# A decoder block whose output projection goes from seven products of halves to plain products by column tiles

## The chip, the cores and the metric

The kernel runs as one program on one core of a Trainium2 chip. The metric is the device time of one execution in microseconds (us). Engines are named as in the profile: PE (TensorE) multiplies, PEld is its loading of weights, DVE is VectorE, ACT is ScalarE, POOL is GpSimd, and SP issues the transfers (DMA).

## The reference

One decoder layer over 1024 tokens of width 1024. An input projection feeds three groups of token mixers (sparse attention with 8 heads of 64, a convolution of 256 channels, gated linear attention of 256 values). Their results, 1024 columns in all, go through ONE output projection and are added to the residual stream; then come a gated FFN of width 2816, a gated embedding and a last norm. The part that matters here:

```
x = x + concatenate([y_nsa, y_conv, y_gla]) @ w_out         # 1024 x 1024 @ 1024 x 1024
h = rms_norm(x, ffn_norm_g)                                 # x * rsqrt(mean(x*x) + eps) * g
x = x + (silu(h @ ffn_w_gate) * (h @ ffn_w_up)) @ ffn_w_down
```

## The kernel before

**Layout and precision.** The residual stream is held transposed: 8 tiles of 128 rows (columns of the model) by 1024 tokens. A float32 operand is split in a high part (a cast on ACT, L1043) and a low part (a subtraction, L271, on VectorE, or on POOL while the counter `pool_lo` is above 0), and every product of two operands is three matmuls: high x high (L1054), high x low (L1055), low x high (L1056). `split` (L1041) makes such a pair of parts from 128 x 512 values. A "product" of the text is one such 128 x 128 by 128 x 512 matmul.

**Seven products for eight.** The output projection works on pairs of column tiles, the two halves of the inner dimension (4 tiles of 128 each) and the two halves of the tokens, as 2 x 2 blocks, and forms seven block products in place of eight from sums and differences of blocks. `Right` (L1058) makes the seven operands on the token side ("11", "21", "22" and the sums "t1" to "t4", 4 splits each; t1, t2 and t4 are subtracted in place on VectorE, t3 on POOL). `Pair` (L1079) loads two tiles of weights, makes the weight sums on POOL (L1105 and L271) and the seven block products of 12 matmuls each, in four banks, with copies of intermediate results (L1095, L1116, L1126, L1135) and sums of them on POOL (L1136, L1137). `residual` (L1163) then adds the blocks to x, with 3 additions on VectorE and 4 on POOL for each pair (L1169), stores x, squares it on ACT (L1187) and adds the squares to sqs, one half on VectorE and one on POOL, and scales x by the norm's gain (L1190) to a "raw" tile, in place for the first three pairs. The FFN's gate and up projections use the same two classes, with the raws as the right side: `Right(raws[:4], raws[4:])` after the projection, then "11", the first product of two pairs, "t1", the fifth product, "21", and so on.

**Order.** The inner dimension is turned round so that the convolution and the linear attention come first (tiles 0 to 3, loaded from a buffer `ycg`) and the attention heads last (tiles 4 to 7). `out_steps` (L1146) is a generator that is advanced while the last units of attention drain: it makes "11", the first products of two pairs, "t1" and the fifth products, 48 matmuls that need only tiles 0 to 3. After attention come a third pair's first product, "21", the second products, and the rest. The instructions of every engine are put in order ahead of time by a scheduler, which may take a later instruction first when it is ready, so that operands of the FFN are begun while the projection still runs. The order of each engine is then fixed. Tiles live in a set of 46 slots of 4 KB for each partition (and four smaller ones), assigned by a dry run of the program; eight banks of PSUM are used in turn.

Of the kernel before, what the change touches and what calls it, by code (L numbers as in the profile page):

```python
# [12 lines left out]
AF = mybir.ActivationFunctionType  # L13
ALU = mybir.AluOpType
# [6 lines left out]
P = 128  # L21
NT = S // P
KT = D // P
# [59 lines left out]
RINGS = ((0, 3), (3, 7), (7, 8))  # L83
LOOK = 3
EARLY = 2
SQE = "vp"
RES = "pppp"
DPL = 7
D3 = True
RAWIN = 3  # L90
FIFTH = 2
DEPTH = 3
LATE = (2, 1, 1)
# [129 lines left out]
def tile_block(ctx: ExitStack, tc: tile.TileContext, a: dict, out: bass.AP, plan: Plan):  # L223
    nc = tc.nc
    mm = nc.tensor.matmul
# [17 lines left out]
    def B(name, dt=F32, shape=(P, 1024)):  # L243
        return place(name, shape, dt)
# [4 lines left out]
    def M(n, shape, dt=F32):  # L249
        return place(f"m{n}", shape, dt)  # L250
# [42 lines left out]
    pv = {n: par[:, s:e] for n, (s, e) in PAR.items()}  # L293
# [127 lines left out]
    ycg = dram.tile([4, P, S], F32, name="ycg")  # L421
# [120 lines left out]
    ps = mtile(4)  # L542
# [122 lines left out]
    for i in range(2):  # L665
        ps = mtile(5 + i)
# [54 lines left out]
    for t in range(NT):  # L721
        ps = row_tile(wV, 280, t)
        if t % 2 == 0:
            V.append(B("V", F32R, (P, 2, 4, P)))
        v = V[-1][:, t % 2]
# [141 lines left out]
    for br in range(2):  # L867
        ps = B("kv")
# [172 lines left out]
    def split(src):  # L1041
        o = B("op", F32R, (P, 2, 512))
        nc.scalar.copy(o[:, 0, :], src)  # L1043
        sub(nc.gpsimd if pool_lo[0] > 0 else nc.vector, o[:, 1, :], src, f(o[:, 0, :]))
        pool_lo[0] -= 1
        return o

    def half(x, n):
        return x[:, n * 512:(n + 1) * 512]
# [8 lines left out]
    class Right:  # L1058
# [5 lines left out]

        def make(self, *names):
            for k, (l, u) in enumerate(zip(self.lower, self.upper)):
                b11, b12, b21, b22 = half(l, 0), half(l, 1), half(u, 0), half(u, 1)
                for n in names:
                    if n == "t1":
                        sub(nc.vector, b11, b12, b11)  # L1070
                    if n == "t2":
                        sub(nc.vector, b11, b22, b11)
                    if n == "t3":
                        sub(nc.gpsimd, b12, b22, b12)
                    if n == "t4":
                        sub(nc.vector, b11, b21, b11)
                    self.x[n][k] = split({"21": b21, "22": b22, "t3": b12}.get(n, b11))
# [63 lines left out]

    x1d = dram.tile([KT, P, S], F32, name="x1d")
    actd = dram.tile([MF, P, S], F32, name="actd")
    outs = []

    def out_steps():  # L1146
        for kt in range(4, 8):
            nats[kt] = B("nat")
            nc.sync.dma_start(out=nats[kt], in_=ycg[kt - 4])
        r = Right([nats[4 + k] for k in range(4)], [nats[k] for k in range(4)])  # L1150
        outs.append(r)
        pool_lo[0] = DPL
        r.make("11")
        for c in range(2):
            outs.append(Pair(a["w_out"], 2 * c, r))
            outs[-1].first(False)
            yield
        r.make("t1")
        for p in outs[1:3]:
            p.fifth()  # L1160
            yield

    def residual(p, c):  # L1163

        for u in range(2):
            m = 2 * c + u
            x = B("x1")
            nc.sync.dma_start(out=x, in_=a["xT"][m])
            add = lambda eng, o, i: eng.tensor_tensor(out=o, in0=i, in1=o, op=ALU.add)  # L1169
            x0, x1_ = half(x, 0), half(x, 1)  # L1170
            if u == 0:
                add(nc.vector, x0, p.a)
                add(nc.vector, p.p6, p.c)
                add(by[RES[0]], x1_, p.p6)
            else:
                add(nc.vector, p.p1, p.b)
                add(by[RES[1]], x0, p.p1)
                add(by[RES[2]], p.p5, p.p67)
                add(by[RES[3]], x1_, p.p5)
            nc.sync.dma_start(out=x1d[m], in_=x)  # L1180
            if m == 0:
                sqs.append(B("sqs"))
                nc.scalar.activation(sqs[0], x, AF.Square)
            else:
                for k in range(2):
                    sq = M(2, (P, 512))
                    nc.scalar.activation(sq, half(x, k), AF.Square)  # L1187
                    add(by[SQE[k]], half(sqs[0], k), sq)
            raws.append(x if c < RAWIN else B("raw"))
            nc.scalar.activation(raws[m], x, AF.Copy, scale=pv["ffng"][:, m:m + 1])  # L1190

    raws, sqs = [], []
    by = {"v": nc.vector, "p": nc.gpsimd}

    nxt = iter(())
    pend = []
# [26 lines left out]
        products(*fifo.pop(0))  # L1223
    pump(og)
    pool_lo[0] = 0
    r = outs.pop(0)
    if D3:
        outs.append(Pair(a["w_out"], 4, r))
        outs[-1].first(False)
    r.make("21")  # L1230
    for p in outs:
        p.second()
    r.make("t2")
    outs[0].sixth()
    r.make("t3", "22", "t4")
    for c in range(KT // 2):
        if c >= len(outs):
            outs.append(Pair(a["w_out"], 2 * c, r))
            outs[c].first()
        outs[c].rest()  # L1240
        residual(outs[c], c)


    r = Right(raws[:4], raws[4:])
    r.make("11")
    pairs = {}
    for q in range(EARLY):
        pairs[q // 2, q % 2] = Pair(a["w_u" if q % 2 else "w_g"], q // 2 * 2, r)
        pairs[q // 2, q % 2].first(False)
    r.make("t1")  # L1250
    for q in range(FIFTH):
        pairs[q // 2, q % 2].fifth()
    r.make("21")
# [65 lines left out]
    def add(o, i0, eng=nc.vector):  # L1319
        eng.tensor_tensor(out=o, in0=i0, in1=o, op=ALU.add)  # L1320
# [244 lines left out]
```

## Time and profile before

| | |
|---|---|
| median of 3 runs | 1473.82 us (1468.57 to 1473.93) |
| profiled execution, its time | 1475.02 us |
| profiled execution, its span | 1473.2 us |
| mean granted TensorE clock | 0.975 |
| busy share PE / PEld / DVE / ACT / POOL | 95 / 79 / 73 / 47 / 58% |
| bytes moved | 118.37 MB, 80 GB/s |

The span runs from the first to the last instruction; the execution's own time is 1.8 us longer. A busy share is an average over all stages. A matmul's own time (about 0.4 us) is longer than the distance to the next one, as matmuls are pipelined; the distance is what counts. The granted clock is a share of 2.4 GHz.

### The profile page before, as it was taken

Reading aid. Unit: us, or ns where it says so; the run is one execution under the profiler, and the core shown is the slowest. Engines: PE = TensorE matmul, PEld = TensorE weight load, DVE = VectorE, ACT = ScalarE, POOL = GpSimd, SP = SyncE. Lnnn points to the kernel's source line nnn. Section 1 sums busy time; section 2 is a strip of 40 time slices with the busy share of each in tenths; the row PEclk is TensorE's granted clock in tenths of the full one; section 3 lists DMA queues with packets and bytes.
Section 4 is the critical chain, followed back from the end, with each engine's and each line's share of the span. In section 5 each row is a group of like instructions: output and inputs, shape, how many; then the busy total and the mean of one; then the engine's idle time right before and its main releaser. Section 6 shows DMA issues by size and latency. Waiting matters only on the chain.

```text
span 1473.2 us, 19463 instructions
## 1 busy us (share of the span) xinstructions
PE 1393.6 (95%) x7032; PEld 1166.6 (79%) x7032; DVE 1072.9 (73%) x1767; ACT 687.5 (47%) x1337; POOL 849.6 (58%) x778
## 2 busy tenths in 40 slices
PE   8999999999999989878899999999996999999998
PEld 6898777889998977756688888888874877876886
DVE  3896548468998978698766666566659999988533
ACT  7322522448887876554433333333334343544532
POOL 3850533548887785986565556665678659423111
PEclk9999999999999999987999999999999999999999
DMA  9101022400000031421222221222263522221211
GB/s 359 56 15 48 26 67 69 148 0 9 5 5 8 2 119 43 172 100 43 72 86 86 86 73 70 73 87 86 86 236 115 182 94 78 105 93 46 69 54 43
DMA packets 40783, 118.37 MB, mean 80 GB/s; under 512 B 4532, under 2 KB 9326, under 8 KB 40686
## 3 DMA queue, kind: packets, MB, share of 16 engines
q1 hardware_dynamic: 40542, 117.11, 22.9%
q8 instruction: 55, 0.90, 0.3%
q14 instruction: 42, 0.34, 0.1%
q10 hardware_dynamic: 144, 0.01, 0.0%
HBM read 94.03 MB, written 23.08 MB: 79 GB/s over the span
## 4 chain that ended last, share of the span: by engine, by line
PE 61%; DVE 17%; POOL 10%; ACT 4%; issue 4%; DMA 3%; SPq 0%; POOLq 0%; DVEq 0%; ACTq 0%
DVE op L271 10%; PE banks L1054 6%; PE banks L1056 6%; PE banks L1055 6%; PE banks L970 3%; PE banks L375 3%; PE banks L376 3%; PE banks L372 3%; POOL st L271 3%; ACT op L1043 3%; PE banks L1014 2%; PE banks L1015 2%; PE banks L910 2%; PE banks L1462 2%; PE banks L1460 2%
## 5 line engine op out<-in xcount | busy, mean ns | idle before, releaser
L1054 PE MATMUL banks<-op 128*128 128x512 f32 x728 | 285.5, 399 | 20.4 <-ACT op L1043 10.4
L1055 PE MATMUL banks<-op 128*128 128x512 f32 x728 | 288.8, 397 | 5.4 <-DVE op L271 5.4
L1056 PE MATMUL banks<-op 128*128 128x512 f32 x728 | 284.8, 397 | 3.1 <-DVE op L271 3.0
L1410 PE MATMUL banks<-op 128*128 128x512 f32 x924 | 220.4, 398 | 23.2 <-DVE x L1320 10.2
L1410 PEld LDWEIGHTS banks<-op 128*128 128x128 f32 x924 | 175.8, 192 | 67.3 <-DVE op L271 10.5
L271 DVE TENSOR_TENSOR op<-nat,op 128x512 fp32r<-128x512 f32 x179 | 176.1, 1001 | 46.1 <-ACT op L1043 44.0
L1043 ACT CAST op<-nat 128x512 fp32r<-128x512 f32 x186 | 111.7, 620 | 178.7 <-DVE op L271 82.8
L1054 PEld LDWEIGHTS banks<-op 128*128 128x128 f32 x728 | 139.4, 192 | 55.0 <-ACT op L1043 13.4
L1056 PEld LDWEIGHTS banks<-op 128*128 128x128 f32 x728 | 139.5, 192 | 35.4 <-DVE op L271 6.2
L1055 PEld LDWEIGHTS banks<-op 128*128 128x128 f32 x728 | 139.8, 192 | 34.8 <-DVE op L271 5.9
L271 DVE TENSOR_TENSOR op<-ws,op 128x512 fp32r<-128x512 f32 x104 | 109.4, 1057 | 78.4 <-ACT op L1043 76.1
L925 POOL TENSOR_SCALAR p<-p,sums,gates 128x640 f32<-128x640 f32 (+7 forms) x128 | 99.9, 791 | 38.6 <-DVE sums L921 29.0
L1043 ACT CAST op<-ws 128x512 fp32r<-128x512 f32 x104 | 63.8, 620 | 108.5 <-POOL ws L271 74.7
L916 ACT ACTIVATE p<-p,mn 128x640 f32<-128x640 f32 (+7 forms) x128 | 94.7, 742 | 11.8 <-DVE mn L913 11.7
L372 PE MATMUL banks<-hT,whi 128*128 128x512 f32 x208 | 84.7, 408 | 6.9 <-ACT hT L328 6.4
L375 PE MATMUL banks<-hT,whi 128*128 128x512 f32 x208 | 84.4, 406 | 0.5 <-DVE hT L329 0.5
L376 PE MATMUL banks<-hT,wlo 128*128 128x512 f32 x208 | 83.0, 401 | 0.0
L970 PE MATMUL banks<-cst,p 128*128 128x128 f32 x448 | 72.1, 279 | 6.8 <-DVE pt L271 4.5
L271 DVE TENSOR_TENSOR op<-st,op 128x512 fp32r<-128x512 f32 x66 | 70.4, 1080 | 9.4 <-ACT op L1043 8.5
L1043 ACT CAST op<-st 128x512 fp32r<-128x512 f32 x66 | 39.7, 619 | 78.4 <-POOL st L271 51.7
L271 DVE TENSOR_TENSOR pt<-banks,pt 128x512 fp32r<-128x512 f32 (+1 forms) x114 | 64.0, 570 | 9.7 <-ACT pt L981 8.6
L910 PE MATMUL banks<-k,qst 128*128 128x512 f32 (+2 forms) x192 | 68.6, 363 | 1.0 <-POOL qst L271 0.5
(303 smaller groups left out, 3369.6 us busy)
## 6 DMA issues: line engine op xcount, KB each, us to landing
nat<-in_w_g SPq DMA_DIRECT2D x22, 512.0 KB, 3.2
nat<-in_w_u SPq DMA_DIRECT2D x22, 512.0 KB, 3.6
actd<-sg SPq DMA_DIRECT2D x22, 512.0 KB, 3.0
nat<-in_w_d SPq DMA_DIRECT2D x22, 512.0 KB, 5.8
nat<-actd SPq DMA_DIRECT2D x22, 512.0 KB, 4.3
nat<-in_w_t SPq DMA_DIRECT2D x13, 512.0 KB, 4.3
xT<-in_xT SPq DMA_DIRECT2D x16, 256.0 KB, 5.8
x<-in_x SPq DMA_DIRECT2D x8, 512.0 KB, 8.0
```

What stands on the lines that cost most here:

```text
L271: return eng.tensor_tensor(out=o, in0=i0, in1=i1, op=ALU.subtract)
L372: r = mm(o, hi[:, w], x[:, 0, :], start=kt == 0, stop=False)
L375: mm(o, hi[:, w], x[:, 1, :], start=False, stop=False)
L376: mm(o, lo_[:, w], x[:, 0, :], start=False, stop=kt == KT - 1)
L910: mark("pe", mm(ps[:, :max(w, 256)], q, kdup[br][g][:, k], start=True, stop=False))
L925: nc.gpsimd.tensor_scalar(out=ps_out[br][:, :n], in0=ps_out[br][:, :n], scalar1=sums[:, br:br + 1], scalar2=gates[:, qb, 3 * head(h) + 1 + ...
L970: nc.tensor.transpose(ps[:, (2 * m + e) * P:(2 * m + e + 1) * P], blk(e, kb, br, ka), ident)
L1043: nc.scalar.copy(o[:, 0, :], src)
L1054: mm(ps, w[:, 0, c], x[k][:, 0, :], start=start and k == 0, stop=False, skip_group_check=True)
L1055: mm(ps, w[:, 0, c], x[k][:, 1, :], start=False, stop=False, skip_group_check=True)
L1056: mm(ps, w[:, 1, c], x[k][:, 0, :], start=False, stop=k == 3, skip_group_check=True)
L1410: mm(groups[g][t], r[:, v, c], l[:, u, :], start=start and (i, u, v) == (0, 0, 0), stop=i == len(ops) - 1 and u == 1, skip_group_check=True)
```

## The change

The output projection computes each of the 8 column tiles on its own: 8 inner tiles x 2 halves of the tokens x 3 matmuls, in two banks. `out_steps` does this for column tiles 0 and 1 with the inner tiles 0 to 6; inner tile 7 follows after attention, then column tiles 2 to 7 in full. `residual` works on one column tile: two additions out of the banks on VectorE, the store of x, the scaled copy into a tile of its own, the square written over x, and one addition of 1024 columns to sqs on VectorE; the squares of tile 0 are sqs itself. The FFN's first two right operands, "11" and "t1", are made after column tile 4, from the first four raws. The number of low parts that POOL is given at the end of attention goes from 7 to 4.

```diff
@@ -83,11 +83,7 @@
 RINGS = ((0, 3), (3, 7), (7, 8))
 LOOK = 3
 EARLY = 2
-SQE = "vp"
-RES = "pppp"
-DPL = 7
-D3 = True
-RAWIN = 3
+DPL = 4
 FIFTH = 2
 DEPTH = 3
 LATE = (2, 1, 1)
@@ -1064,7 +1060,8 @@
 
         def make(self, *names):
             for k, (l, u) in enumerate(zip(self.lower, self.upper)):
-                b11, b12, b21, b22 = half(l, 0), half(l, 1), half(u, 0), half(u, 1)
+                b11, b12 = half(l, 0), half(l, 1)
+                b21, b22 = (half(u, 0), half(u, 1)) if u is not None else (None, None)
                 for n in names:
                     if n == "t1":
                         sub(nc.vector, b11, b12, b11)
@@ -1141,56 +1138,63 @@
 
     x1d = dram.tile([KT, P, S], F32, name="x1d")
     actd = dram.tile([MF, P, S], F32, name="actd")
-    outs = []
+    xop, outs = {}, {}
+
+    def out_half(m, hf, kts, first, last):
+
+        ps = outs[m][1][hf]
+        for i, kt in enumerate(kts):
+            w, c = outs[m][0][kt // 4], slice(kt % 4 * P, kt % 4 * P + P)
+            x = xop[kt][hf]
+            mm(ps, w[:, 0, c], x[:, 0, :], start=first and i == 0, stop=False, skip_group_check=True)
+            mm(ps, w[:, 0, c], x[:, 1, :], start=False, stop=False, skip_group_check=True)
+            mm(ps, w[:, 1, c], x[:, 0, :], start=False, stop=last and i == len(kts) - 1, skip_group_check=True)
+
+    def out_weights(m):
+        w = B("nat")
+        nc.sync.dma_start(out=w, in_=a["w_out"][m])
+        outs[m] = [split(half(w, n)) for n in range(2)], [bank(), bank()]
+
+    def operand(kt, src):
+        xop[kt] = [split(half(src, n)) for n in range(2)]
 
     def out_steps():
-        for kt in range(4, 8):
-            nats[kt] = B("nat")
-            nc.sync.dma_start(out=nats[kt], in_=ycg[kt - 4])
-        r = Right([nats[4 + k] for k in range(4)], [nats[k] for k in range(4)])
-        outs.append(r)
+
+        for kt in range(4):
+            nats[4 + kt] = B("nat")
+            nc.sync.dma_start(out=nats[4 + kt], in_=ycg[kt])
         pool_lo[0] = DPL
-        r.make("11")
-        for c in range(2):
-            outs.append(Pair(a["w_out"], 2 * c, r))
-            outs[-1].first(False)
+        for kt in range(4):
+            operand(kt, nats[4 + kt])
+        for m in range(2):
+            out_weights(m)
+            for hf in range(2):
+                out_half(m, hf, range(4), True, False)
             yield
-        r.make("t1")
-        for p in outs[1:3]:
-            p.fifth()
-            yield
-
-    def residual(p, c):
-
-        for u in range(2):
-            m = 2 * c + u
-            x = B("x1")
-            nc.sync.dma_start(out=x, in_=a["xT"][m])
-            add = lambda eng, o, i: eng.tensor_tensor(out=o, in0=i, in1=o, op=ALU.add)
-            x0, x1_ = half(x, 0), half(x, 1)
-            if u == 0:
-                add(nc.vector, x0, p.a)
-                add(nc.vector, p.p6, p.c)
-                add(by[RES[0]], x1_, p.p6)
-            else:
-                add(nc.vector, p.p1, p.b)
-                add(by[RES[1]], x0, p.p1)
-                add(by[RES[2]], p.p5, p.p67)
-                add(by[RES[3]], x1_, p.p5)
-            nc.sync.dma_start(out=x1d[m], in_=x)
-            if m == 0:
-                sqs.append(B("sqs"))
-                nc.scalar.activation(sqs[0], x, AF.Square)
-            else:
-                for k in range(2):
-                    sq = M(2, (P, 512))
-                    nc.scalar.activation(sq, half(x, k), AF.Square)
-                    add(by[SQE[k]], half(sqs[0], k), sq)
-            raws.append(x if c < RAWIN else B("raw"))
-            nc.scalar.activation(raws[m], x, AF.Copy, scale=pv["ffng"][:, m:m + 1])
+        for kt in range(4, 7):
+            operand(kt, nats[kt - 4])
+        for m in range(2):
+            for hf in range(2):
+                out_half(m, hf, range(4, 7), False, False)
+        yield
+
+    def residual(m):
+
+        x = B("x1")
+        nc.sync.dma_start(out=x, in_=a["xT"][m])
+        for hf in range(2):
+            o = half(x, hf)
+            nc.vector.tensor_tensor(out=o, in0=outs[m][1][hf], in1=o, op=ALU.add)
+        nc.sync.dma_start(out=x1d[m], in_=x)
+        raws.append(B("raw"))
+        nc.scalar.activation(raws[m], x, AF.Copy, scale=pv["ffng"][:, m:m + 1])
+        nc.scalar.activation(x, x, AF.Square)
+        if m == 0:
+            sqs.append(x)
+        else:
+            nc.vector.tensor_tensor(out=sqs[0], in0=x, in1=sqs[0], op=ALU.add)
 
     raws, sqs = [], []
-    by = {"v": nc.vector, "p": nc.gpsimd}
 
     nxt = iter(())
     pend = []
@@ -1223,31 +1227,23 @@
         products(*fifo.pop(0))
     pump(og)
     pool_lo[0] = 0
-    r = outs.pop(0)
-    if D3:
-        outs.append(Pair(a["w_out"], 4, r))
-        outs[-1].first(False)
-    r.make("21")
-    for p in outs:
-        p.second()
-    r.make("t2")
-    outs[0].sixth()
-    r.make("t3", "22", "t4")
-    for c in range(KT // 2):
-        if c >= len(outs):
-            outs.append(Pair(a["w_out"], 2 * c, r))
-            outs[c].first()
-        outs[c].rest()
-        residual(outs[c], c)
-
-
-    r = Right(raws[:4], raws[4:])
-    r.make("11")
+    operand(7, nats[3])
+    for m in range(KT):
+        if m > 1:
+            out_weights(m)
+        for hf in range(2):
+            out_half(m, hf, range(7, 8) if m < 2 else range(8), m > 1, True)
+        residual(m)
+        if m == 4:
+
+            r = Right(raws[:4], [None] * 4)
+            r.make("11")
+            r.make("t1")
+    r.upper = raws[4:]
     pairs = {}
     for q in range(EARLY):
         pairs[q // 2, q % 2] = Pair(a["w_u" if q % 2 else "w_g"], q // 2 * 2, r)
         pairs[q // 2, q % 2].first(False)
-    r.make("t1")
     for q in range(FIFTH):
         pairs[q // 2, q % 2].fifth()
     r.make("21")
```

## Rows read from the trace of the kernel before

**Rows 1.** the page, part 1: busy time and share of each engine

```profile
PE 1393.6 (95%) x7032; PEld 1166.6 (79%) x7032; DVE 1072.9 (73%) x1767; ACT 687.5 (47%) x1337; POOL 849.6 (58%) x778
```

**Rows 2.** by stretch: busy us (records) PE, PEld, DVE, ACT, POOL; clock; DMA; GB/s

```profile
526.00:563.00 37.00, 28.73 (x160) 24.69 (x159) 27.37 (x43) 23.35 (x52) 34.22 (x27) 0.82 0.29 107
563.00:608.00 45.00, 45.00 (x214) 37.41 (x213) 35.87 (x48) 27.71 (x49) 27.49 (x19) 1.00 0.29 103
608.00:740.00 132.00, 106.41 (x408) 82.90 (x408) 109.75 (x107) 64.83 (x109) 97.46 (x73) 0.87 0.24 84
634.50:700.00 65.50, 47.89 (x168) 37.50 (x169) 59.15 (x59) 34.24 (x59) 47.61 (x40) 0.77 0.20 72
```

**Rows 3.** timeline of PE at full rate, 753 to 758 us

```profile
753.41 0.39 PE L1054 MATMUL banks<-op 128*128 128x512 f32 x1
...
758.17 0.39 PE L1054 MATMUL banks<-op 128*128 128x512 f32 x1
```

**Rows 4.** costliest groups, shapes apart, PE, 608 to 740 us

```profile
L1054 PE MATMUL banks<-op 128*128 128x512 f32 x130 | 56.3, 436 | 17.2 <-ACT op L1043 8.7 <-ACT cp L1126 8.1 <-ACT cp L1095 0.3
L1055 PE MATMUL banks<-op 128*128 128x512 f32 x129 | 55.4, 430 | 5.4 <-DVE op L271 5.4
L1056 PE MATMUL banks<-op 128*128 128x512 f32 x129 | 53.9, 427 | 3.0 <-DVE op L271 3.0
```

**Rows 5.** waits of PE, 608 to 740 us: us in total, times, longest

```profile
PE banks L1054 <- ACT op L1043: 8.7, 4, 3.9
PE banks L1054 <- ACT cp L1126: 8.1, 1, 8.1
PE banks L1055 <- DVE op L271: 5.4, 2, 4.3
PE banks L1056 <- DVE op L271: 3.0, 2, 2.4
```

**Rows 6.** timeline of DVE, 635 to 656 us

```profile
635.90 3.42 DVE L271 TENSOR_TENSOR x<-x 128x512 f32<-128x512 f32 x2
...
650.55 1.76 DVE L271 TENSOR_TENSOR x<-x,x 128x512 f32<-128x512 f32 x1
652.23 0.68 DVE L271 TENSOR_TENSOR op<-x,op 128x512 fp32r<-128x512 f32 x1
...
654.64 0.68 DVE L1169 TENSOR_TENSOR x<-banks,x 128x512 f32<-128x512 f32 x1
```

**Rows 7.** timeline of POOL, 648 to 656 us

```profile
650.04 1.71 POOL L271 TENSOR_TENSOR ws<-nat 128x512 f32<-128x512 f32 x1
654.19 1.68 POOL L271 TENSOR_TENSOR ws<-ws,nat 128x512 f32<-128x512 f32 x1 [2.44 <-DVE op L271]
```

**Rows 8.** timeline of ACT, 620 to 643 us

```profile
622.61 0.62 ACT L1043 CAST op<-x 128x512 fp32r<-128x512 f32 x1
...
637.73 0.62 ACT L1043 CAST op<-x 128x512 fp32r<-128x512 f32 x1 [5.01 <-DVE x L271]
...
641.90 0.56 ACT L1126 COPY cp<-banks 128x512 f32<-128x512 f32 x1
```

**Rows 9.** costliest groups, shapes apart, operands and residual, 608 to 740 us

```profile
L271 DVE TENSOR_TENSOR op<-x,op 128x512 fp32r<-128x512 f32 x24 | 26.4, 1124 | 0.1
...
L1169 POOL TENSOR_TENSOR x<-cp,x 128x512 f32<-128x512 f32 x9 | 15.3, 1703 | 5.5 <-DVE cp L1169 5.5
...
L1169 POOL TENSOR_TENSOR sqs<-m,sqs 128x512 f32<-128x512 f32 x7 | 12.0, 1709 | 0.0
...
L1190 ACT ACTIVATE x<-x,par 128x1024 f32<-128x1024 f32 x5 | 5.7, 1149 | 1.5 <-DMA x1d<-x 1.5
...
L1169 DVE TENSOR_TENSOR cp<-banks,cp 128x512 f32<-128x512 f32 x4 | 2.7, 677 | 0.0
```

**Rows 10.** DMA issues, 590 to 740 us: KB each, us to landing

```profile
x1d<-x SPq DMA_DIRECT2D x8, 512.0 KB, 3.4
...
nat<-in_w_out SPq DMA_DIRECT2D x2, 512.0 KB, 4.5
```

## The prediction

> **What bounds the kernel now.** The page's busy shares come first: PE is busy for 1393.6 of the 1473.2 us of the span, 95% [rows 1]. Whoever stops there expects the change to cost what it adds on PE. The share is a mean over stages, so the stretches around the output projection come next [rows 2]. From 526 to 563 us, the end of attention, PE is busy for 28.73 of 37.0 us at a mean granted clock of 0.82. From 563 to 608 us, the middle of the output projection, it is never idle. From 608 to 740 us, where the projection ends and the FFN begins, it is busy for 106.41 of 132.0 us at a clock of 0.87.
>
> To see what 608 to 740 us loses, PE's rate is needed. Undisturbed, 21 products lie between the starts at 753.41 and 758.17 us [rows 3]: 4.76 / 21 = 0.227 us each. The stretch holds 130 + 129 + 129 = 388 products [rows 4], or 88 us of work; the other 20 of its 408 records [rows 2] are small products of the norm, some 4 us at most, and a few missing records may hide 2 us more. So 132 - 94 = **38 us** are lost: 25.6 us of idle time, and the rest in products at the lower of the two clock levels (1.2 instead of 2.4 GHz), since the mean granted clock of 0.87 lies between them.
>
> The table of waits says for what PE is idle [rows 5]: ACT's casts (8.7 us), one copy on ACT (8.1 us, once) and VectorE's low parts (5.4 and 3.0 us). ACT is not the cause. In its timeline a cast of an FFN operand stands idle for 5.01 us for the subtraction on VectorE that makes it, and the copy L1126 is behind that cast [rows 8]. VectorE is at 59.15 of 65.5 us from 634.5 to 700 us [rows 2]. **VectorE's operand work is the bound there**, not PE.
>
> VectorE is slow there for a reason that two timelines show together. A subtraction of two SBUF tiles took 1.76 us at 650.55, when POOL was in an addition of 1.71 us that began at 650.04; at 652.23, in POOL's pause of 2.44 us, the same form took 0.68 us; at 654.64, with POOL at work again, an addition whose one input is a PSUM bank took 0.68 us [rows 6, 7]. So POOL's tensor additions cost VectorE's two-tile operations about 1.1 us each, and its reads of banks nothing.
>
> **The change, part by part.**
>
> *Products.* A pair of column tiles takes 7 x 12 products now and 8 x 12 then. Four pairs: 336 become 384, **48 more at 0.227 us, +10.9 us**. They lie on the path wherever PE is dense, so I count them all.
>
> *Work beside PE in the projection.* The now 28 operand splits and 28 weight splits become 16 and 16; the sums t1 to t4 (16), the weight sums (16, on POOL), the sums of products (8, on POOL), and 16 of the 28 residual additions, those on POOL, go. That POOL work was the slowing one: nine additions on x alone took 15.3 us and the seven on sqs 12.0 us between 608 and 740 [rows 9]. Per column tile there is left on VectorE two weight splits (0.68 us each in POOL's pause), two additions out of banks (0.677 us each, [rows 9]) and one addition of squares, 1024 wide with both inputs in SBUF. No row has that width; by two 512-wide ones it is 1.4 us with POOL quiet and 3.5 us beside POOL. I take 1.4, as POOL is nearly empty then. Together 4.1 us, at worst 8.4. On ACT: two casts (0.62 each, [rows 8]), the scaled copy (1.15, [rows 9]) and the square of the same width, some 3.5 us. A tile takes 48 x 0.227 = 10.9 us on PE. **I cost this work at nothing**: PE covers it even at the worst.
>
> *The FFN's first operands.* "11" and "t1" (12 VectorE operations) are now made from the first four raws after column tile 4, so they go beside three tiles or 33 us of PE, of which VectorE needs 3 x 4.1 for residuals and weights. They cost nothing; without that cover they would be 12 x 1.1 us, the mean of the operand splits [rows 9], or 13 us.
>
> *What stays behind the last column tile.* "21", "t2", "t3", "22" and "t4" need the last four raws: 4 + 8 + 4 + 4 + 8 = 28 VectorE operations, and some six weight splits of the first FFN pairs, 34 in all. PE's cover until the last of them is needed is products 1, 5 and 2 of two pairs, then 6, 3 and the one with "22" of the first: 9 x 12 x 0.227 = 24.5 us. At 0.68 us each the chain is 23 us and costs nothing; at 1.76 us, every operation beside POOL, it is 60 us and PE loses 35. I take 1.124 us, the mean of the same splits now [rows 9], because POOL still makes the FFN's weight sums and the "t3" differences in this stretch: 38.2 - 24.5 = **14 us stay of the 38**. Products at half rate inside this time are no extra, since PE waits for the chain anyway. Gain 24 us.
>
> *The end of attention.* It loses 8.3 us idle and, at a mean clock of 0.82, some 5 us more, 13 in all [rows 2]. The early products grow from 48 to 84 and need 18 splits in place of 12 splits, 4 subtractions and 4 POOL sums; only 4 of the splits are offered to POOL instead of 7. More filling for PE, slightly more on VectorE: **I take 0**, between -12 (all filled) and +5 (VectorE later for the attention's own transposes).
>
> *Queues.* SP issues the same loads of weights and x and the same stores; each weight tile (4.5 us to land, [rows 10]) has a tile's 10.9 us ahead of it. The new wait is on ACT: the square is written over x, so it waits until the store of x has read it (3.4 us to land, [rows 10]), and casts behind it wait too. The scaled copy, now in place, has waited so for 1.5 us in all [rows 9]. Cost 0 if the next tile's casts are ahead of it; otherwise see the second rival.
>
> **The sum** is made against the profiled execution, 1475.0 us: + 10.9 - 24 + 0 = -13, or 1462. The median of the three runs is 1.2 us lower than that execution, so the forecast for it is **1461 us**, with 1453 to 1467 as its own range.
>
> The Trainium skill, "SBUF — State Buffer", section "SBUF: two separate sides", says that a VectorE operation with two SBUF inputs and a GpSimd operation that reads SBUF take turns at one port, and the second waits for the whole of the first. By that rule an operation that meets POOL costs 0.68 us plus up to POOL's own duration, and the sum would be the first rival's if POOL never pauses; the rows agree in kind (1.76 against 0.68 us).
>
> **The rivals.**
>
> *The chain is not relieved (slower).* The place is the FFN's start: if POOL's sums for the first two FFN pairs fall together with the 28 operand operations, each takes 1.76 us and 35 of the 38 us stay. Then 1475.0 + 10.9 - 3 = 1483; own range 1479 to 1490. It decides at about 1.5 us per operation: there the chain is 51 us, 27 us stay, and the 11 us saved are the 10.9 us of the products. For it: the weight splits in this stretch run beside POOL today, and the 5.01 us wait is in the FFN's own operands, not in the projection's. Against it: the additions that filled POOL are gone [rows 9], and operands of raws 4 to 6 can be made before the last tile, as FFN casts already began at 622.61 us, far ahead of the FFN's products [rows 8].
>
> *ACT is held by the square (no change).* If the casts for tile m+1 stand behind the square of tile m, PE waits from the end of tile m for two additions (1.4), the store (3.4), the square (1.15), a cast (0.62) and a low part (0.68): 7.3 us. Two such tiles of six give 1461 + 15 = 1476; own range 1467 to 1481. Against it: the order is planned ahead, and ACT's 3.5 us a tile leave it time.
>
> The Trainium skill, "TensorE: Matmul & The Clock Gate", section "Part 1: The HAM clock gate", calls ACT a strict FIFO. This rule speaks against the change; the cast at 637.73 that holds up the copy L1126 [rows 8] agrees with it.
>
> *The end of attention fills too (faster still).* The 36 more early products enter its gaps and 12 of its 13 us go: 1449.
>
> **How the numbers follow.** Forecast 0.44, chain not relieved 0.28, ACT held 0.18, attention filled 0.10. Half a per cent (7.4 us) is about what a measurement of this kernel can tell from no change. The forecast (0.42 of its 0.44) and the filled attention are faster: 0.52. Held ACT, the forecast's upper rim and the lower rim of the unrelieved chain give 0.23 for no change; the rest of the chain's rival is slower, 0.25. The range goes from 1447, just under the filled attention, to 1484, over most of the unrelieved chain.
>
> **What would show it.** Right: 384 products at 0.227 us with PE dense from the end of attention to the last column tile; VectorE's subtractions near 0.7 us in the projection; POOL nearly idle there; PE's waits at the FFN's start down from 25 us to 10 or so. Wrong: VectorE at 1.7 us and over 90% busy for 40 us behind the last tile (first rival), or ACT idle for x1d stores with PE waiting for its casts (second rival).

## The result, and the profile after

| | before | after |
|---|---|---|
| median (four runs each) | 1472.74 us | 1448.88 us (1443.36 to 1450.37) |
| profiled execution, its span | 1473.2 us | 1441.6 us |
| ratio after / before | | **0.9832**, interval 0.9814 to 0.9850 |

The change is faster by 24 us. The sign was forecast and the time lies in the range, but the forecast gain was 12 to 13 us: half of what came. One caution for the two profiles: after's is the shortest of its runs, and it is ahead before the changed code begins (the loads of `ycg` are issued at 516.47 us, before at 522.01 us; in the kernels of the experiments that follow, at 516.56 to 521.95 us). Some 5 us of the 31.6 us between the spans are therefore not the change's, and the comparisons below go by stages and by ratios.

Busy time and share of each engine, page of after, part 1:

```profile
PE 1387.6 (96%) x7080; PEld 1163.3 (81%) x7080; DVE 1028.8 (71%) x1738; ACT 665.6 (46%) x1290; POOL 765.6 (53%) x724
```

The 48 added products are there (7032 to 7080), and POOL lost 54 operations and 84 us against [rows 1]. By stretch (busy us and records of PE, PEld, DVE, ACT, POOL; clock; DMA share; GB/s):

```profile
520.50:557.50 37.00, 31.99 (x176) 27.11 (x175) 20.04 (x39) 22.00 (x49) 16.44 (x14) 0.91 0.30 103
...
563.00:608.00 45.00, 45.00 (x225) 38.15 (x224) 27.23 (x42) 22.44 (x33) 3.70 (x3) 1.00 0.54 188
608.00:740.00 132.00, 123.81 (x534) 98.61 (x533) 94.03 (x105) 56.66 (x92) 68.30 (x56) 0.99 0.19 68
```

The first stretch is before's 526 to 563 us, moved by the 5.5 us: PE is busy for 31.99 of 37 us at a clock of 0.91, against 28.73 at 0.82 [rows 2]; how much of that the change makes is asked further down. In 608 to 740 us it is busy for 123.81 us at 0.99, against 106.41 at 0.87. Its groups there:

```profile
L1052 PE MATMUL banks<-op 128*128 128x512 f32 x129 | 51.4, 401 | 0.4 <-DVE op L267 0.4
L1050 PE MATMUL banks<-op 128*128 128x512 f32 x130 | 51.3, 400 | 6.9 <-ACT op L1039 4.2 <-ACT cp L1132 1.5 <-ACT cp L1092 0.9
...
L1150 PE MATMUL banks<-op 128*128 128x512 f32 x42 | 16.3, 389 | 0.0
```

With the groups left out (one of the FFN with 130, two of the projection with 42 and 41), 514 products ran here. Counted as in the prediction, 514 x 0.227 = 116.7 us, plus 4 for the norm's small products and 2 for missing records: 132 - 122.7 = **9 us are lost, where 38 were**. What PE still waits for (total, times, longest):

```profile
PE banks L1050 <- ACT op L1039: 4.2, 1, 4.2
PE banks L1050 <- ACT cp L1132: 1.5, 1, 1.5
PE banks L1050 <- ACT cp L1092: 0.9, 1, 0.9
PE banks L1051 <- DVE op L267: 0.7, 1, 0.7
```

Each wait of [rows 5] is gone or small but one: the 4.2 us come at 732 us, in the steady FFN, and have their twin before (3.89 us at 729.25 us). VectorE's groups in the same stretch, and its timeline behind the last column tile, whose last product starts at 635.80 us:

```profile
L267 DVE TENSOR_TENSOR op<-raw,op 128x512 fp32r<-128x512 f32 x20 | 16.2, 849 | 0.1
...
L267 DVE TENSOR_TENSOR raw<-raw 128x512 f32<-128x512 f32 x7 | 5.2, 759 | 2.4 <-ACT raw L1190 2.4
```

```profile
644.21 1.78 DVE L267 TENSOR_TENSOR op<-raw,op 128x512 fp32r<-128x512 f32 x1
645.92 0.68 DVE L267 TENSOR_TENSOR raw<-raw 128x512 f32<-128x512 f32 x1
646.52 0.68 DVE L267 TENSOR_TENSOR op<-raw,op 128x512 fp32r<-128x512 f32 x1
647.12 1.28 DVE L267 TENSOR_TENSOR raw<-raw 128x512 f32<-128x512 f32 x2
648.33 3.08 DVE L267 TENSOR_TENSOR op<-raw,op 128x512 fp32r<-128x512 f32 x5
...
657.51 1.46 DVE L267 TENSOR_TENSOR op<-ws,op 128x512 fp32r<-128x512 f32 x2
```

And POOL's timeline beside it:

```profile
643.63 1.82 POOL L267 TENSOR_TENSOR raw<-raw 128x512 f32<-128x512 f32 x1 [0.50 <-ACT raw L1190]
645.39 0.20 POOL L337 MEMSET dg<- 128x128 f32 x1
655.70 0.21 POOL L337 MEMSET dg<- 128x128 f32 x1 [10.11 <-DVE raw L267]
```

This is the heart of the result. While POOL was in its subtraction of 643.63 us, VectorE's operation took 1.78 us; from 645.6 to 655.7 us POOL stood idle, and VectorE made its operands at 0.6 to 0.7 us each. In the kernel before POOL had hardly a pause there [rows 7]. The sums of weights, which I had expected beside these operands, had mostly been made between 625 and 637 us.

### The profile page after: what moved, and what is told of

Its sections match the earlier page's. It is cut to its first block, busy times and chain, and to the rows that moved or that the text cites. A ratio compares the mean times of both kernels' runs of the same rounds, so it can differ in the third digit from the quotient of the medians.

```text
span 1441.6 us, 19394 instructions
## 1 busy us (share of the span) xinstructions
PE 1387.6 (96%) x7080; PEld 1163.3 (81%) x7080; DVE 1028.8 (71%) x1738; ACT 665.6 (46%) x1290; POOL 765.6 (53%) x724
## 4 chain that ended last, share of the span: by engine, by line
PE 52%; DVE 17%; POOL 12%; DMA 7%; issue 6%; ACT 5%; SPq 0%; POOLq 0%; DVEq 0%; ACTq 0%
DVE op L267 10%; PE banks L1406 6%; POOL ws L267 4%; PE banks L966 3%; PE banks L371 3%; PE banks L372 3%; PE banks L368 3%; ACT op L1039 3%; PE banks L1010 2%; PE banks L1011 2%; DMA nat<-in_w_u 2%; PE banks L906 2%; PE banks L1456 2%; PE banks L1457 2%; PE banks L1458 2%
## 5 line engine op out<-in xcount | busy, mean ns | idle before, releaser
L1050 PE MATMUL banks<-op 128*128 128x512 f32 x616 | 237.1, 393 | 8.2 <-ACT op L1039 4.2
L1051 PE MATMUL banks<-op 128*128 128x512 f32 x616 | 240.5, 391 | 0.7 <-DVE op L267 0.7
L1406 PE MATMUL banks<-op 128*128 128x512 f32 x924 | 222.6, 402 | 18.4 <-DVE x L1316 6.6
L1052 PE MATMUL banks<-op 128*128 128x512 f32 x616 | 238.9, 392 | 0.6 <-DVE op L267 0.4
L1406 PEld LDWEIGHTS banks<-op 128*128 128x128 f32 x924 | 178.1, 194 | 62.6 <-DVE x L1316 9.4
L267 DVE TENSOR_TENSOR op<-nat,op 128x512 fp32r<-128x512 f32 x174 | 162.0, 949 | 57.1 <-ACT op L1039 55.5
L1039 ACT CAST op<-nat 128x512 fp32r<-128x512 f32 x178 | 106.3, 620 | 179.1 <-DVE op L267 64.7
L1050 PEld LDWEIGHTS banks<-op 128*128 128x128 f32 x616 | 116.0, 188 | 37.3 <-ACT op L1039 5.1
L267 DVE TENSOR_TENSOR op<-ws,op 128x512 fp32r<-128x512 f32 x88 | 89.9, 1026 | 73.4 <-ACT op L1039 71.3
L1052 PEld LDWEIGHTS banks<-op 128*128 128x128 f32 x616 | 115.9, 188 | 27.3 <-DVE op L267 2.7
L1051 PEld LDWEIGHTS banks<-op 128*128 128x128 f32 x616 | 116.1, 188 | 24.9 <-DVE op L267 1.1
L1039 ACT CAST op<-ws 128x512 fp32r<-128x512 f32 x88 | 54.3, 620 | 101.1 <-POOL ws L267 74.7
L267 DVE TENSOR_TENSOR op<-st,op 128x512 fp32r<-128x512 f32 x66 | 77.9, 1199 | 5.6 <-ACT op L1039 5.4
```

The costliest lines, as they stand in the source:

```text
L267: return eng.tensor_tensor(out=o, in0=i0, in1=i1, op=ALU.subtract)
L1050: mm(ps, w[:, 0, c], x[k][:, 0, :], start=start and k == 0, stop=False, skip_group_check=True)
L1051: mm(ps, w[:, 0, c], x[k][:, 1, :], start=False, stop=False, skip_group_check=True)
L1052: mm(ps, w[:, 1, c], x[k][:, 0, :], start=False, stop=k == 3, skip_group_check=True)
L1406: mm(groups[g][t], r[:, v, c], l[:, u, :], start=start and (i, u, v) == (0, 0, 0), stop=i == len(ops) - 1 and u == 1, skip_group_check=True)
```

## The experiments

Twelve kernels ran, in four groups; a ratio is always to the kernel before on the same chip. "us" made of a difference of ratios takes 1470 us as one.

**1. Is it POOL's additions?** The kernel before, with the residual additions and both halves of the squares on VectorE; nothing else is changed, VectorE has 23 operations more and PE the same products.

```diff
-SQE = "vp"
-RES = "pppp"
+SQE = "vv"
+RES = "vvvv"
```

> The kernel before, with the 16 residual additions and the 7 half squares that POOL did given to VectorE; products and operands stay. If POOL's additions were the cost (they slow VectorE from 0.68 to 1.76 us an operation), POOL loses some 38 us of additions around the projection and VectorE gets 23 operations of 0.7 us more: a good part of the 38 us lost from 608 to 740 us comes back, 1473 becomes 1460 to 1468. If the amount of VectorE's operand work was the cost, 23 more operations make it worse: 1476 to 1485. Either way 336 products in the projection.

Ratio 0.9929 (0.9914 to 0.9943): 10 us faster, although VectorE was given more to do. Its groups and its stretches show why:

```profile
L271 DVE TENSOR_TENSOR op<-x,op 128x512 fp32r<-128x512 f32 x24 | 17.3, 742 | 2.3 <-ACT op L1043 2.3
```

```profile
563.00:608.00 45.00, 40.57 (x174) 31.77 (x172) 41.38 (x52) 24.72 (x42) 22.12 (x13) 1.00 0.34 117
608.00:740.00 132.00, 116.72 (x472) 91.61 (x473) 106.15 (x131) 69.36 (x115) 83.15 (x58) 0.92 0.22 80
```

The group of 24 splits that took 1124 ns each [rows 9] takes 742 ns, and PE gains 10 us of busy time in 608 to 740 us. The price is 4.4 us in the stretch before it, which was dense. One rival this run leaves open: the residual's own chain is shorter too, when an addition of 1.7 us on POOL becomes one of 0.68 us on VectorE. The second experiment does not have it, as nobody reads the results of its additions.

**2. The same at the FFN's start alone.** The kernel after, with 16 POOL additions put back beside the FFN's first operands. Six of them start before the projection's last product (638.93 us in this run), ten behind it. Nobody reads their results.

```diff
     r.upper = raws[4:]
+    for k in (5, 5, 5, 5, 6, 6, 6, 6, 7, 7, 7, 7, 7, 7, 7, 7):
+        nc.gpsimd.tensor_tensor(out=M(2, (P, 512)), in0=half(raws[k], 0), in1=half(raws[k], 1), op=ALU.add)
```

> The kernel after with 16 GpSimd additions of two 128x512 SBUF tiles put back beside the FFN's first operands (as many as the nine on x and seven on sqs that ran between 608 and 740 us before); nobody reads their results, and TensorE's products are those of the kernel after. Theory: the operands behind the last column tile cost 0.85 us each in the kernel after, and not the 1.124 us of the prediction, only because GpSimd pauses beside them. Then VectorE's op<-raw goes back to 1.1 us or more, TensorE waits 10 to 20 us more between 608 and 740 us, and the time is 1460 to 1470 us, 0.991 to 0.998. Rival: the count of VectorE's operations decides, or GpSimd's own sums run late for another reason; then op<-raw stays under 0.95 us, and the ratio at 0.983 to 0.987.

Ratio 0.9931 (0.9912 to 0.9950), 1459.97 us: (0.9931 - 0.9832) x 1470 = **15 us of the gain are given back**. VectorE and POOL between 608 and 740 us, PE's wait, and PE's two stretches 636 to 680 and 680 to 740 us:

```profile
L267 DVE TENSOR_TENSOR op<-raw,op 128x512 fp32r<-128x512 f32 x20 | 23.1, 1193 | 0.8 <-ACT op L1039 0.7
```

```profile
L1244 POOL TENSOR_TENSOR m<-raw 128x512 f32<-128x512 f32 x16 | 27.7, 1751 | 12.8 <-ACT raw L1190 12.8
```

```profile
PE banks L1051 <- DVE op L267: 9.3, 1, 9.3
```

```profile
636.00:680.00 44.00, 32.81 (x130) 25.92 (x129) 41.39 (x39) 18.82 (x33) 31.77 (x23) 0.84 0.07 24
680.00:740.00 60.00, 58.85 (x251) 46.35 (x250) 41.56 (x44) 23.31 (x37) 38.31 (x34) 1.00 0.20 71
```

The 20 operand splits go from 849 to 1193 ns, with the same count. PE's idle time between 608 and 740 us grows by only 4 us (12.3 against 8.2), less than was expected, though after's holds the 4.2 us of 732 us, whose twin (3.8 us) comes behind 740 us here. Counted by work and not by idle time the loss is there: PE has 130 records in 636 to 680 us at a clock of 0.84, where after has 187 at 1.00, and 57 x 0.227 = 13 us. The rival, that the number of VectorE's operations decides, falls for this place. The size holds for additions placed as here; before, some of the 16 came earlier.

**3. Parts of the change, one by one.** Each is the kernel after but for one thing.

The FFN's first operands written behind the loop, as in the kernel before:

```diff
-        if m == 4:
-            r = Right(raws[:4], [None] * 4)
-            r.make("11")
-            r.make("t1")
-    r.upper = raws[4:]
+    r = Right(raws[:4], raws[4:])
+    r.make("11")
...
+    r.make("t1")
```

> The kernel after, but the FFN's right operands are written down as before: all of them after the projection's loop, t1 behind the first products. If the place after column tile 4 was the gain (operands made beside the last three tiles), 12 operations of 1.1 us go back to the FFN's start: 1449 becomes 1459 to 1463. If the planned order takes them early anyway, as it did before the change (first FFN cast at 622.61 us), it stays at 1446 to 1452.

0.9834 (0.9818 to 0.9851): no difference. The casts of the raws begin at 587.23 us, in after at 586.37 us: the scheduler takes them early wherever they are written.

48 early products, those of inner tiles 0 to 3 alone, in place of 84:

```diff
-        for kt in range(4, 7):
-            operand(kt, nats[kt - 4])
-        for m in range(2):
-            for hf in range(2):
-                out_half(m, hf, range(4, 7), False, False)
-        yield
```

> The kernel after, with 48 early products as before in place of 84: inner tiles 4 to 6 of column tiles 0 and 1 wait until attention has drained. If the 36 more products filled gaps at the end of attention, which fell by some 6 us, 1449 becomes 1454 to 1457. If those gaps went because of the lighter operand work (no t1 differences, no weight sums on POOL), it stays at 1447 to 1451.

0.9838 (0.9825 to 0.9851): no difference. The better end of attention does not come from more products to fill it with.

The squares by halves, one of them on POOL, as before:

```diff
+                (nc.gpsimd if k else nc.vector).tensor_tensor(out=o, in0=sq, in1=o, op=ALU.add)
-            nc.vector.tensor_tensor(out=sqs[0], in0=x, in1=sqs[0], op=ALU.add)
```

> The kernel after, with the squares as before: two halves, one added on VectorE and one on POOL, sqs in a tile of its own. If this second part of the change matters by itself, 7 additions on POOL of 1.3 to 1.7 us slow VectorE beside them by 1.1 us each, up to 8 us: 1453 to 1457. If PE covers the residual's work in the projection, as forecast, it stays at 1446 to 1452.

0.9856 (0.9842 to 0.9870): some 3.5 us, anything from 0 to 8 us by the ends of the two intervals, which overlap, so that this part of the change is not settled as a gain of its own. Six of the seven POOL additions start here before the projection's last product, where PE's products cover VectorE, and one behind it; in the second experiment ten lie behind it.

The price of products: the 48 of column tile 5 issued twice, the first time into banks that are started again.

```diff
+            if m == 5:
+                out_half(m, hf, range(8), True, False)
```

> The kernel after, with the 48 products of column tile 5 issued twice (the second time from the start of the banks): the price of 48 products by itself. If PE is the bound in the projection, as its dense stretch of 83 us says, the price is 48 x 0.227 = 10.9 us: ratio to the kernel before 0.983 + 0.0074 = 0.991, the profile's span 1452 to 1457. If waits nearby would take the products in, less than 5 us more: ratio under 0.987.

0.9884 (0.9864 to 0.9903): 0.0052 x 1470 = 7.7 us, and between 2 and 13 us by the ends of the two intervals. The ratio lies between the two forecasts; the 10.9 us of the prediction are inside the interval. The trace is sharper: the projection's last product starts at 648.35 us, after's at 635.80 us, with the loads of `ycg` 1.3 us later here, so 11.2 us later; PE has no gap from 552 to 646 us. In this stretch the products cost their full price.

The number of low parts that POOL is given, 7 as before and not 4:

```diff
-DPL = 4
+DPL = 7
```

> The kernel after, with 7 low parts offered to POOL at the end of attention as before, in place of 4. If the shorter gaps there come from POOL being given less, some 3 us come back: ratio 0.985 to 0.986. If not, 0.983 to 0.984.

0.9841 (0.9819 to 0.9863): no difference in the time, which could not tell 2 us; what its trace shows at the end of attention stands in the section on the forecast.

**4. How far does it go?** First the kernel before with POOL out of the projection altogether: residual, squares, sums of weights, sums of products and "t3" there all on VectorE.

```diff
-SQE = "vp"
-RES = "pppp"
+SQE = "vv"
+RES = "vvvv"
...
-                        sub(nc.gpsimd, b12, b22, b12)
+                        sub(peng[0], b12, b22, b12)
...
-            nc.gpsimd.tensor_tensor(out=self.s, in0=self.a21, in1=self.a22, op=ALU.add)
+            peng[0].tensor_tensor(out=self.s, in0=self.a21, in1=self.a22, op=ALU.add)
...
+    peng[0] = nc.gpsimd
     r = Right(raws[:4], raws[4:])
```

(`peng[0]` is VectorE up to the FFN's operands; the other lines of `Pair` change alike.)

> The kernel before, seven products for eight, with all of the projection's additions on VectorE: beside the residual's and the squares' also the 16 weight sums, the 8 sums of products and the 4 differences t3. If turns with POOL were all of the loss, it gains on 0.993: 0.986 to 0.990. If the amount of operand work takes over once POOL is out of the way, 28 operations of 0.7 us more on VectorE make it slower than 0.993: 0.996 to 1.002.

0.9953 (0.9935 to 0.9971): in neither of the two ranges, no better than the residual and squares alone (0.9929), and likely worse, as the intervals hardly overlap. Its stretches:

```profile
563.00:608.00 45.00, 39.63 (x166) 31.09 (x167) 38.17 (x63) 24.20 (x42) 0.00 (x0) 0.94 0.37 125
608.00:740.00 132.00, 116.10 (x467) 91.45 (x467) 103.04 (x138) 68.50 (x114) 74.62 (x49) 0.92 0.21 77
```

POOL does nothing from 563 to 608 us and PE still loses 5.4 us there, with 63 VectorE operations in place of 48 [rows 2]. So POOL is not all of it with the seven-product scheme. That the *quantity* of operand work is the next bound fits (VectorE has 138 operations in 608 to 740 us, in after 105) but is argued, not shown: VectorE's operations take 0.68 us each from 563 to 608 us and it is busy for 38.17 of 45 us, and 3.6 of the 5.4 us come at 602 to 605 us, behind a wait of 2.02 us in which VectorE stands idle for the load of x. So the order of the work is a rival that no run separates. Plain products need less of this work and put less of it on POOL; after is ahead of both variants of before.

Then the same step in the down projection, which the change did not touch: its 88 sums of weights and of operands go from POOL to VectorE, in the kernel after.

```diff
-                nc.gpsimd.tensor_tensor(out=x.s, in0=x.a21, in1=x.a22, op=ALU.add)
-                sub(nc.gpsimd, x.t, x.b12, x.b11)
+                nc.vector.tensor_tensor(out=x.s, in0=x.a21, in1=x.a22, op=ALU.add)
+                sub(nc.vector, x.t, x.b12, x.b11)
```

(and the six other lines of `operands` alike)

> The kernel after, with the 88 sums of operands of the FFN's down projection on VectorE in place of POOL. VectorE is at 93 to 98% there and its low parts take 1.199 us in the mean beside POOL; PE loses some 18 us in that stage. If POOL's additions are what makes VectorE slow, 88 operations of 0.65 us come to VectorE and 88 waits of about 1.1 us go: VectorE is relieved, 3 to 12 us faster, ratio 0.975 to 0.981. If the number of VectorE's operations is what counts, 55 us more on an engine that is full already: 30 us slower or more.

0.9764 (0.9741 to 0.9786), 0.7% under after. Two groups of VectorE from 1050 to 1345 us, first in after, then here:

```profile
L267 DVE TENSOR_TENSOR op<-nat,op 128x512 fp32r<-128x512 f32 x89 | 79.2, 913 | 0.9
L267 DVE TENSOR_TENSOR op<-st,op 128x512 fp32r<-128x512 f32 x66 | 77.9, 1199 | 5.6 <-ACT op L1039 5.4
```

```profile
L267 DVE TENSOR_TENSOR op<-nat,op 128x512 fp32r<-128x512 f32 x89 | 59.3, 691 | 0.0
L267 DVE TENSOR_TENSOR op<-st,op 128x512 fp32r<-128x512 f32 x66 | 44.9, 690 | 0.0
```

155 splits cost 157.1 us in after and 104.2 us here. The 53 us saved pay for most of the added sums (88 at 0.68 us are 60 us): VectorE does all of POOL's work almost for nothing. In the same stretch one POOL addition took 11.29 us at 1068 us (below), ahead of a wait of PE of 7.4 us. Three kernels ask whether sums of the FFN should move as well: those of the last pair of raws' products, of the first and last, of all pairs. Each moves the two sums in `Pair.rest`, the c22 addition and POOL's multiplication, over and above the run just shown:

```diff
-            nc.gpsimd.tensor_tensor(out=self.p6, in0=self.p6, in1=self.p1, op=ALU.add)
-            nc.gpsimd.tensor_tensor(out=self.p67, in0=self.p67, in1=self.p1, op=ALU.add)
+            peng[0].tensor_tensor(out=self.p6, in0=self.p6, in1=self.p1, op=ALU.add)
+            peng[0].tensor_tensor(out=self.p67, in0=self.p67, in1=self.p1, op=ALU.add)
...
+        peng[0] = nc.vector if c == MF // 2 - 1 else nc.gpsimd
```

> The kernel after with the 88 operand sums of the down projection on VectorE, as in the run before this one of that kind (0.976 of the kernel before), and the last pair of raw FFN products' sums, the c22 addition and the multiplication behind them on VectorE too. If TensorE's 7.4 us wait at the start of the down projection comes from the one GpSimd addition that took 11.29 us beside VectorE's row of additions, then no GpSimd addition of that length is left there, the wait falls below 3 us, and the time is 3 to 7 us less: 0.971 to 0.974. If the wait is the operand work of the first down product itself, whoever does it, the wait stays between 6 and 9 us and the ratio at 0.975 to 0.978.

0.9763 (0.9737 to 0.9788): nothing gained. The long addition is gone, but PE waits 5.9 us in the same stage (a figure that neither side had named), for VectorE's `x` instead. The theory that the time is lost by POOL's 11.29 us addition falls.

> The same, and the first pair's sums, c22 addition and multiplication on VectorE as well, where one VectorE subtraction took 6.79 us beside a row of GpSimd operations. If that subtraction held TensorE (its waits of 635 to 740 us sum to some 8 us), 2 to 4 us less than the run with the last pair alone: 0.969 to 0.973. If TensorE had products in hand meanwhile, the same within 0.1%.

0.9741 (0.9717 to 0.9764): 3 us, inside the uncertainty and in neither range. From 635 to 740 us PE is busy for 101.54 us, in the run before this one for 97.11, so the gain is likely there.

> The same for all pairs: GpSimd keeps only the sums of weights in the FFN. If what costs is GpSimd and VectorE sharing, it is as fast as the run with first and last pair or faster, 0.966 to 0.972, and VectorE's subtractions in the steady FFN take near 0.68 us. If VectorE's quantity of work limits (as it did where the whole projection went to VectorE before the change), it is slower than the run with first and last pair by over 0.5%: 0.976 or more.

**0.9683 (0.9660 to 0.9707), 1426.53 us**: the fastest kernel of the study, 46 us under before and 22 us under after. Two of its stretches:

```profile
635.00:740.00 105.00, 103.33 (x459) 84.40 (x458) 89.65 (x114) 51.65 (x87) 39.18 (x37) 1.00 0.20 70
740.00:1050.00 310.00, 308.87 (x1363) 255.25 (x1362) 228.28 (x294) 119.19 (x196) 94.00 (x65) 1.00 0.24 85
```

In the first one PE is busy for 103.33 of 105 us; after has 96.81 there. In the second, VectorE takes 69 operations more than in after (294 against 225) at 33 us more busy time and PE stays dense. VectorE is at 74% there, so there was room. Its splits did not fall to 0.68 us as I had expected (0.83 to 0.91 us; POOL keeps the sums of weights). Between the spans of this run and of after lie 14 us, and 5.5 more, as this run issues the loads of `ycg` that much later (521.95 us): 19.7 us to account for. The two places give 8.5: 6.5 us in the first and 9 more records (2 us) in the second. Most of the rest is in the down projection, which this run shares with the run on its 88 sums: from 1050 to 1345 us PE has 1203 records here, 1207 there and 1164 in after, and 39 x 0.227 = 8.9 us. Some 2 us are not located.

## Why the forecast had the sign and half the size

**Where PE was held: right.** The forecast took VectorE's operand work beside POOL for the bound of 608 to 740 us, and not PE. Experiment 1 shows it in the kernel before (more work on VectorE, 10 us less), experiment 2 in the kernel after.

**The step that failed: "I take 1.124 us, the mean of the same splits now ... because POOL still makes the FFN's weight sums and the "t3" differences in this stretch: 38.2 - 24.5 = 14 us stay of the 38."** The count was good: 34 operations were forecast behind the last column tile, and 31 ran there between 635.77 and 658.97 us (25 for the raws, 6 of weights). The price was not: 23 us for the chain, 0.75 us each (two operations of the residual, 1.9 us, included), where 38.2 us were forecast. With 24.5 us of cover it costs PE next to nothing, two waits for low parts of 1.1 us in all, as the prediction's own lower end had it. The 9 us that remain are mostly other waits, above all the 4.2 us at 732 us. So of the 14 us that were to stay for this chain hardly any did, other waits that the prediction had at nothing took 8 or so, and the net error of the term is 5 us, 9 against 14. The error is one of consistency. The 1.124 us were a mean from the kernel before, taken while the 27.3 us of POOL additions of [rows 9] ran beside these splits, and the step before had just taken those additions away. Experiment 2 puts 16 of them back: 1193 ns and 15 us. The first rival, the chain not relieved, is the same error at its far end.

**The end of attention, "I take 0": too low by some 3 us that the traces show.** Stretches from 510 to 570 us, in the order before, the first experiment, after, and after with 7 low parts:

```profile
510.00:570.00 60.00, 51.73 (x324) 46.09 (x323) 47.12 (x100) 39.82 (x94) 49.18 (x45) 0.89 0.25 90
510.00:570.00 60.00, 52.07 (x324) 46.14 (x323) 52.31 (x93) 43.09 (x93) 49.52 (x40) 0.94 0.25 91
510.00:570.00 60.00, 54.99 (x334) 48.11 (x333) 37.80 (x82) 36.80 (x82) 26.63 (x26) 0.94 0.35 117
510.00:570.00 60.00, 53.04 (x331) 46.74 (x331) 36.84 (x85) 36.34 (x83) 29.95 (x30) 0.94 0.33 109
```

PE stood idle for 8.3 us before and does so for 5.0 in after. The clock went from 0.89 to 0.94, some 2.6 us of work, but the first experiment has 0.94 as well, and its edit lies behind this stretch: that part is not shown to be the change's. The 36 early products are not the cause (the run without them loses 5.6 us). The number of low parts may be a part of it: with 7 PE's idle time is 7.0 us. POOL's lighter load (26.63 against 49.18 us) as the cause is argued, not shown: in the kernel before with the projection off POOL its load is 33.92 us and PE is still idle for 8.4 us, with more work on VectorE. The third rival foresaw a gain here and a time of 1449 us, which is the time measured. That is coincidence: its mechanism (more filling) is ruled out by the 48-products run, and most of the gain came from the other place.

**Products, +10.9 us: right.** By the time 7.7 us (2 to 13), by the trace of the projection 11.2 us.

**Work beside PE in the projection, nothing: right.** From 563 to 608 us PE is busy for 45.00 us, and VectorE for 27.23.

**ACT held by the square: the wait came, the loss did not.** ACT's timeline in the projection:

```profile
608.17 1.06 ACT L1191 ACTIVATE x<-x 128x1024 f32<-128x1024 f32 x1 [2.71 <-DMA x1d<-x]
...
619.64 1.06 ACT L1191 ACTIVATE x<-x 128x1024 f32<-128x1024 f32 x1 [3.30 <-DMA x1d<-x]
```

The square does wait for the store of x, and PE has no gap beside it, since the casts for the next tiles were ahead in the order.

**The sum**, corrected: +10.9 - 29 - 3 gives -21 us, and -24 was measured (0.9832; 22 to 27 by the interval). Of the 11 us that the forecast's -13 lacks, 5 are the price of the chain and 3 the end of attention; some 3 stay open, of the size of the clock's part there.

## What to carry to other kernels

Before moving element-wise work to GpSimd to relieve VectorE, look at how long VectorE's operations with two SBUF inputs take beside it: here each addition that VectorE met cost it some 1.1 us, more than the 0.68 us in which it does one itself, and taking additions back from GpSimd made VectorE's own work cheaper at the FFN's start, in the down projection and in the FFN. It does not go on for ever: where all of the old projection's additions went to VectorE, nothing more was gained. When a forecast prices what is left, take the duration from a stretch that looks as the new kernel will (here the 0.68 us of POOL's pause), not from the mean of a stretch that holds the very work that goes.

## What the runs showed of the hardware that was not expected

Two engines did not always take turns one operation at a time. In the run with the down projection's sums on VectorE, POOL's timeline has

```profile
1068.27 11.29 POOL L1133 TENSOR_TENSOR cp<-cp 128x512 f32<-128x512 f32 x1 [7.60 <-ACT cp L1123]
1079.52 1.28 POOL L1134 TENSOR_TENSOR cp<-cp 128x512 f32<-128x512 f32 x1
```

and VectorE's, over the same time, a row of two-input operations without a pause:

```profile
1068.36 0.68 DVE L1337 TENSOR_TENSOR st<-nat 128x512 f32<-128x512 f32 x1
1068.96 0.68 DVE L267 TENSOR_TENSOR op<-st,op 128x512 fp32r<-128x512 f32 x1
...
1077.72 0.68 DVE L267 TENSOR_TENSOR nat<-nat 128x512 f32<-128x512 f32 x1
1082.20 0.69 DVE L1268 TENSOR_TENSOR cp<-cp,rbc 128x512 f32<-128x512 f32 x1 [3.79 <-POOL cp L1267]
```

An addition that takes 1.28 us when it runs alone (the next one did) ended 1.2 us after VectorE's row (1079.56 against 1078.40 us), as if it had begun when the row was over, and VectorE then stood idle for 3.79 us for POOL. The other way round, in the kernel after, VectorE and then POOL:

```profile
668.29 6.79 DVE L267 TENSOR_TENSOR op<-nat,op 128x512 fp32r<-128x512 f32 x1 [3.25 <-ACT op L1039]
```

```profile
668.26 1.29 POOL L1102 TENSOR_TENSOR ws<-nat 128x512 f32<-128x512 f32 x1
...
673.26 1.27 POOL L1267 TENSOR_TENSOR sg<-cp 128x512 f32<-128x512 f32 x1
```

A subtraction that elsewhere takes 0.68 us lasted as long as five POOL operations behind each other. That the one waits for the other is read from the overlap in time; no run varied it. The Trainium skill, "SBUF — State Buffer", section "SBUF: two separate sides", says that whichever of the two starts first has the port for its whole instruction and the other is blocked. The rows agree in kind, and seem to go further: the one that is blocked can wait through a whole row of the other's instructions, 11.29 us here, not through one.
